# Hyena filters and delta gates: products over 16, 33 and 64 rows made over 128 rows, two passes over the gates' rows made one

## The chip, the cores and the metric

The kernel runs on one core of a Trainium2 chip. The metric is the device time of one execution in microseconds (us); three runs give a median and a spread. PE is TensorE, DVE VectorE, ACT ScalarE, POOL GpSimd, SP the engine whose queue carries the weights' transfers.

## What is computed

Two model blocks follow each other on 256 tokens of 1024 features. The first has two layers, each a gated feed-forward half step, a mixer and a second feed-forward half step. The second has an even mixer with an MLP and an odd mixer with an MLP, and takes a context stream of 256 tokens beside the latent one. The change touches the odd mixer alone. Its two halves are a long convolution whose filters come out of a small network of sines, and a gated delta rule:

```python
def hyena_filters(length, w1, b1, freq1, w2, b2, freq2, w3):
    ...                                           # z: [length, 33]
    hid = jnp.sin(freq1 * (z @ w1 + b1))          # 33 -> 64
    hid = jnp.sin(freq2 * (hid @ w2 + b2))        # 64 -> 64
    filt = (hid @ w3).astype(F32).reshape(length, HY_ORDER, 2, HY_CH)
    filt = filt * jnp.exp(-t * deltas)[:, None, None, :]
    return filt / jnp.sum(jnp.abs(filt), axis=(0, 2), keepdims=True)

def gated_delta_chunked(q, k, v, beta, g, state):   # 4 heads, chunks of 64, both directions
    gcum = jnp.cumsum(g, axis=-1)
    decay = jnp.exp(jnp.where(incl, gcum[..., :, None] - gcum[..., None, :], -jnp.inf))
    lower = jnp.where(strict, jnp.einsum('bhncd,bhnsd->bhncs', kb, k) * decay, 0.0)
    tmat = lax.linalg.triangular_solve(eye + lower, ...)
    ...
    attn = jnp.einsum('bhncd,bhnsd->bhncs', q, k) * decay
```

## The kernel before

Activations lie with the features on the partitions and the tokens on the free axis. A float32 product is made of three float32r passes, high part by high part, high by remainder and remainder by high (`mm3`, L634 to L638). The weights stream once in chunks of six 128x128 tiles: SP's queue brings a chunk into one of four `raw` buffers, ACT rounds it to the high part `whi` (L415), DVE subtracts to get the remainder `wlo` (L416). `whi` and `wlo` have four buffers each (NSPLIT), so ACT can write a chunk's high part only when PE has finished with the chunk four places ahead of it. In the odd mixer a chunk is 18 products where it serves the latent stream.

`hyena_filters` is woven into the second feed-forward layer of the first block, by steps. Both layers of sines (L1404) multiply weights `w1` and `w2` on the partitions 0 to 32 and 0 to 63 alone. The last layer's weights `w3` and the hidden values `hs` stand twice, on the lower and on the upper 64 partitions, with high part and remainder so placed that one pass over 128 rows makes two of the three products; a second pass over 64 rows (L1435) adds the third.

In the odd mixer `delta_gates` makes the running sums `gc` of the gates by token for both streams, transposes them for each stream to 16 rows (block, direction, head; L1562) and copies those to `gcT`. `prep` of each stream (L1609 to L1660) spreads them to four heads' columns of their own (`G`), splits these into `Gh` and `Gl`, and yields. Then for each of two blocks and two directions it makes a row of sums stand on all partitions: a pass with `Gh` (L1634), one with `Gl` (L1635), each over 16 rows, and one with an identity that adds the triangle's mask `fb` (L1636). ACT takes exponentials of the result, four 128x128 tiles `A` (and four `w` in the latent stream).

Each stage of the odd mixer is a generator. The recurrence's are chained as main: `prep1`, then `solve1` and `prep0` by turns, then inverses and states by turns, and `output` at last. The features (projections, short convolutions, SiLU, normalisation) and the long convolution are the filler. `fill` (L361) traces after main's i-th step as many filler steps as the i-th digit of `OD_FILL` says, and what is left at the end. A scheduler then sets each engine's order from what is traced. ACT holds one table of functions at a time, so in its row an exponential behind a SiLU has an ACT_TABLE_LOAD ahead of it, and a SiLU behind an exponential another.

Of the kernel before, what the change touches and what calls it, by code (L numbers as in the profile page):

```python
"""Two model blocks on one core.

Activations live transposed: features on partitions, tokens on the free axis, so the output of
one product is the moving operand of the next. A float32 product is carried by three float32r
passes: each operand is split exactly into a high part (rounded to float32r) and the remainder,
and hi*hi + hi*lo + lo*hi are accumulated in PSUM. Weights stream once from DRAM in the order of
their use. The per-token factor of a root-mean-square norm is applied where a product leaves PSUM.
"""
# [9 lines left out]
F32 = mybir.dt.float32  # L18
F32R = mybir.dt.float32r
AF = mybir.ActivationFunctionType  # L20
ALU = mybir.AluOpType
# [8 lines left out]
CH = 6             # weight tiles of 128x128 in one transfer  # L30
CHM = 4            # the same in the first block's mixers
NRAW, NSPLIT = 4, 4   # transfers and split parts under way
# [6 lines left out]
# parts of the hidden width held on chip at a time  # L39
FFN_PARTS = {(1, 0): 1, (2, 0): 1, (1, 1): 1, (2, 1): 1}  # L40
MLP_PARTS = (4, 2)  # by layer
AHEADW = {"od": 0}  # weight transfers split ahead of their use, by phase (2 otherwise)
ADA = (1.2, 0.8, 1.2)   # steps of the modulation after each of a feed-forward layer's, by layer
AT0 = 4             # first block's attention: the step of the first head's scores,
ATV = 2             # and the steps from a head's scores to its values
# taps of the even mixer's convolution by each engine after a stream's share of its own inputs and of the others
TAPS = ((4.0, 4.0), (2.0, 2.0))
BY = (0, 1, 0, -14)   # the engine of each channel tile; negative: shared, so many taps by the first
MW = 1              # steps from the attention's norm to its transposes
# products traced between the steps of a chain that waits for other engines: so many steps ahead of it and after each  # L50
# of its own; in the even mixer queries, convolution and its outputs between the attention's,
EV_FILL = "2114110100002000031200110015312110300002013"
# in the odd mixer features, long convolution and its outputs between the recurrence's
OD_FILL = ("0000010011200001101310001000000001000100000000000100001011000000000010"
           "00000000001000020001000100000000000011000000001002000010001001114")
FEATS = 8           # steps of the features ahead of the recurrence
BR = (3, 2)         # tiles of each gate of the long convolution ahead of the transform
ODH = 4             # output tiles of the odd mixer that are begun with the long convolution's half
EVH = 2             # the same in the even mixer
SINES = 2           # filters: steps a layer of sines takes,  # L60
HW = 1              # steps from the filters to their transforms,
HF = 1.1            # steps per step of the feed-forward layer
OUTM = 3            # output tiles of the first block's mixers that grow with their inputs,
OUTL = 2            # so many tiles behind
LATE = 2            # output tiles that are begun before the last input tile is there
TS = T + 2         # moving columns with the two of the shift


# ---------------------------------------------------------------- host: layout only
class Cols:  # L70
    """Vectors laid out per partition: a vector of n*128 becomes n columns."""
# [21 lines left out]
def _late(w, ms, ks):  # L93
    """As lins takes them: the last of ks follows the others of the first LATE output tiles."""
    ms, ks = list(ms), list(ks)
    return _blocks(w, ms[:LATE], ks[:-1]) + _blocks(w, ms[:LATE], ks[-1:]) + _blocks(w, ms[LATE:], ks)

# [71 lines left out]
def _tap_cols(w):  # L169
    """[taps, channels] -> [128, channel tile * taps]"""  # L170
    return w.T.reshape(-1, P, w.shape[0]).transpose(1, 0, 2).reshape(P, -1)


def _tlay(x):
    """[tokens, features] -> [128, feature tile, token]"""
    return np.ascontiguousarray(x.T.reshape(-1, P, x.shape[0]).transpose(1, 0, 2))
# [42 lines left out]
def _consts_od():  # L219
# [5 lines left out]
    # allowed entries 0, the others large; i on partitions, j on the free axis  # L225
# [6 lines left out]
    # of the rows (block, direction, head): those of a block and direction, those of a head  # L232
    c["of_bd"] = p[:, None] // 4 == np.arange(4)[None, :]
# [5 lines left out]
def _consts_big():  # L239
    """Over i on partitions and j: allowed entries 0, the others large."""  # L240
    p = np.arange(P)
    le = p[:, None] <= p[None, :]
    return {"f": np.where(le.T, 0.0, 2.0 ** 100), "b": np.where(le, 0.0, 2.0 ** 100)}


def _consts_dft():
    """Real transform of length 512 and its inverse as matrices."""
# [6 lines left out]
    fwd_i[:, 0] = alt                       # row 0 of the imaginary part carries the last frequency  # L254
    c = {}
    dft = np.concatenate([cos, fwd_i], 1)   # [t, 512]
# [9 lines left out]
def _consts_hy():  # L266
    """Transforms of the filters, positional features, decays."""
# [32 lines left out]
def _prep(i):  # L300
    """Arrays of the launch: every one a rearrangement of inputs, or a constant of the shapes."""
# [13 lines left out]
    # second block  # L315
# [33 lines left out]
# ---------------------------------------------------------------- device  # L349
def weave(main, filler, ratio):  # L350
    """Trace main's steps with ratio steps of filler after each; filler goes on behind them."""
    due = 0.0
    for _ in main:
        due += ratio
        while due >= 1.0:
            due -= 1.0
            next(filler, None)
        yield


def fill(main, filler, counts):  # L361
    """Trace main's steps with so many of filler's ahead and after each as the digits of counts say, the rest at last."""
# [7 lines left out]
def both(*gens):  # L370
    """Trace the steps of generators by turns."""
# [14 lines left out]
class Weights:  # L386
    """The stream of 128x128 weight tiles in the order of their use, split on chip ahead of it."""
# [9 lines left out]
    def load(s, n):  # L397
        """The transfers of the chunks before the n-th."""
# [7 lines left out]
    def split(s, n):  # L406
        """The parts of the chunks before the n-th."""
# [12 lines left out]
    def start(s, name):  # L420
        """The phase's first tile comes next."""
# [16 lines left out]
class Split:  # L438
    """An activation operand as high and low float32r parts, [128, tiles, tokens]."""
# [4 lines left out]
    def put(s, nc, k, f):  # L444
        """Split the float32 values f into tile k."""
# [4 lines left out]
class Norm:  # L450
    """x*g split for products, and the per-token factor R (one row, on all partitions).

    With a shift the moving operand has two more columns that hold it: a product's column T is then
    the shift's product, to be added after the factor R.
    """
# [35 lines left out]
    def square(s, k):  # L491
        """The sum of the squares, so far."""
# [11 lines left out]
    def R(s):  # L504
        """Made where it is first asked for, behind the products that were traced before."""
# [6 lines left out]
    def normalise(s):  # L512
        """Of a full norm: the split of x * R * g + shift, a tile at a time."""
# [10 lines left out]
    def apply(s):  # L524
        """Of a plain norm: the factor R, two tiles of x at a time."""
# [5 lines left out]
    def split_all(s, w):  # L531
        """Without the sum of the squares, which is made with R; the first weights w by the way."""
# [6 lines left out]
    def finish(s):  # L539
# [5 lines left out]
        for i, z in enumerate(chain):  # L545
            z.done = n.tp.tile([P, T], F32, tag="R", name="R", bufs=4)
            v = ps[:, i * T:(i + 1) * T]
            if i:
                # the mean square of what the first norm makes
# [8 lines left out]
    def by_token(s):  # L558
        """R with tokens on partitions, a column per block."""
# [9 lines left out]
class Net:  # L569
    def __init__(s, tc, nc, a, at, st):  # L570
# [9 lines left out]
        # the activation table is loaded during the first transfers  # L580
# [31 lines left out]
    def rsqrt(s, v, scale, out=None):  # L612
        """1/sqrt(v*scale + eps)."""
# [9 lines left out]
    def rows(s, rt, d=None):  # L623
        """[128 tokens, blocks] -> PSUM [128, 128 * blocks], the same row of tokens on each partition."""
# [15 lines left out]
    def lin(s, w, sp, ks, ps=None, n=T):  # L640
        """One tile of 128 outputs: [128 features, tokens]."""
# [7 lines left out]
    def lins(s, w, sp, nk, n=T, nm=KD):  # L649
        """nm tiles of outputs, one after the other; see _late."""  # L650
# [11 lines left out]
    def linc(s, w, nrs):  # L662
        """One tile of 128 outputs of the streams' norms with shifts, by one pass over the weights."""
# [10 lines left out]
    def scaled(s, out, ps, nr, func=AF.Identity, scale=1.0):  # L674
        """func(scale * (ps*R + shift)); the shift's product is column T of ps."""
# [11 lines left out]
    def lin_tok(s, w, sp):  # L687
        """512 outputs, tokens on partitions: two blocks of [128 tokens, 512]."""
# [8 lines left out]
    # ---- first block  # L697
# [30 lines left out]
    def consts_of(s, pool, part):  # L728
        """A phase's constants: a function from name to columns."""
# [5 lines left out]
    def rope(s, ps, dst, cosR, sinR, perm):  # L735
        """The first half; the second one, behind the next products, is returned."""
# [14 lines left out]
    def mixer(s, l, nr, nxt):  # L751
        nc, tc = s.nc, s.tc
        w = s.w.start(f"mix_{l}")
        with tc.tile_pool(name=f"mix{l}", bufs=1) as pool, tc.tile_pool(name=f"mixt{l}", bufs=3) as tp:
# [4 lines left out]
            # small inputs  # L759
# [9 lines left out]
            # indexer  # L769
# [3 lines left out]
            nc.scalar.copy(raw, ps)     # 64 rows of the key, 8 of the heads' weights  # L773
# [58 lines left out]
            def select():  # L832
                """One round of eight of the highest scores."""
# [5 lines left out]
            # spatial gating's normalised part  # L839
# [6 lines left out]
            # keys and queries, meanwhile the selection  # L846
# [49 lines left out]
            # attention over the selected keys  # L896
# [86 lines left out]
    # ---- second block  # L983
# [1112 lines left out]
```

## Time and profile before

| | us |
|---|---|
| runs | 2264.89, 2265.63, 2267.83 |
| median | 2265.63 |
| span of the profiled execution | 2263.6 |
| PE busy in it | 2221.3 (98%) |
| DVE busy | 1717.0 (76%) |
| ACT busy | 1295.0 (57%) |
| POOL busy | 76.1 (3%) |

The profiled execution took 2263.6 us by its span, 2.0 us under the median of the runs. PE is busy in 98% of the span and carries 91% of the chain that ended last. Where windows of the profile are shown, each line has the window, its length, the busy time of each engine with the number of instructions, the granted clock of TensorE as a share of 2.4 GHz, and the share of the time in which the DMA engines moved data.

### The profile page before, as it was taken

Reading aid. Unit: us, or ns where it says so; the run is one execution under the profiler, and the core shown is the slowest. Engines: PE = TensorE matmul, PEld = TensorE weight load, DVE = VectorE, ACT = ScalarE, POOL = GpSimd, SP = SyncE. Lnnn points to the kernel's source line nnn. Section 1 sums busy time; section 2 is a strip of 40 time slices with the busy share of each in tenths; the row PEclk is TensorE's granted clock in tenths of the full one; section 3 lists DMA queues with packets and bytes.
Section 4 is the critical chain, followed back from the end, with each engine's and each line's share of the span. In section 5 each row is a group of like instructions: output and inputs, shape, how many; then the busy total and the mean of one; then the engine's idle time right before and its main releaser. Section 6 shows DMA issues by size and latency. Waiting matters only on the chain.

```text
span 2263.6 us, 43627 instructions
## 1 busy us (share of the span) xinstructions
PE 2221.3 (98%) x16752; PEld 2094.1 (93%) x16752; DVE 1717.0 (76%) x3316; ACT 1295.0 (57%) x2475; POOL 76.1 (3%) x114
## 2 busy tenths in 40 slices
PE   8999999999999999999999889999999999999998
PEld 8999899999999999999999867989989898999998
DVE  7877877887688878786768987767764779778565
ACT  6545566655555455675655667625435588437674
POOL 0000000000000000000003800000000000000000
PEclk9999999999999999999999999999999999999999
DMA  7776555776677755466662212456753325224664
GB/s 267 241 229 216 150 160 148 238 213 203 208 239 237 229 176 165 139 206 190 183 186 87 78 43 86 140 166 193 229 174 94 91 66 177 66 62 147 184 185 133
DMA packets 155754, 374.83 MB, mean 166 GB/s; under 512 B 24856, under 2 KB 29720, under 8 KB 155160
## 3 DMA queue, kind: packets, MB, share of 16 engines
q1 hardware_dynamic: 155544, 372.03, 53.2%
q8 instruction: 131, 2.15, 0.4%
q14 instruction: 79, 0.65, 0.1%
HBM read 365.94 MB, written 6.03 MB: 164 GB/s over the span
## 4 chain that ended last, share of the span: by engine, by line
PE 91%; DVE 4%; ACT 3%; DMA 2%; issue 1%; SPq 0%; DVEq 0%; ACTq 0%
PE mm L636 27%; PE mm L637 27%; PE mm L638 27%; DVE ms L1091 1%; DVE wlo L416 1%; DMA raw<-w_ffn 1%; PE ms L1907 1%; PE mm L1882 1%; PE ms L901 1%; PE ms L816 1%; PE ms L1609 1%; PE ms L1700 1%; PE ms L1706 0%; PE ms L743 0%; PE mm L1258 0%
## 5 line engine op out<-in xcount | busy, mean ns | idle before, releaser
L415 ACT ACTIVATE whi<-raw 128x768 fp32r<-128x768 f32 (+1 forms) x840 | 659.0, 787 | 688.5 <-PE mm L637 488.2
L636 PE MATMUL mm<-xh,whi 128*128 128x256 f32 (+1 forms) x3328 | 956.9, 288 | 10.3 <-ACT whi L415 9.4
L638 PE MATMUL mm<-xh,wlo 128*128 128x256 f32 (+1 forms) x3328 | 943.7, 284 | 2.0 <-DVE wlo L416 1.9
L637 PE MATMUL mm<-xl,whi 128*128 128x256 f32 (+1 forms) x3328 | 944.4, 284 | 0.0
L416 DVE TENSOR_TENSOR wlo<-raw,whi 128x768 fp32r<-128x768 f32 (+1 forms) x840 | 746.3, 894 | 260.3 <-ACT whi L415 254.3
L636 PEld LDWEIGHTS mm<-xh,whi 128*128 128x128 f32 x3328 | 633.1, 190 | 23.8 <-ACT whi L415 14.8
L638 PEld LDWEIGHTS mm<-xh,wlo 128*128 128x128 f32 x3328 | 633.3, 191 | 4.2 <-DVE wlo L416 3.7
L637 PEld LDWEIGHTS mm<-xl,whi 128*128 128x128 f32 x3328 | 633.1, 190 | 3.2 <-issue 1.7
L636 PE MATMUL mm<-hh,whi 128*128 128x256 f32 x704 | 197.9, 281 | 0.0
L637 PE MATMUL mm<-hl,whi 128*128 128x256 f32 x704 | 197.6, 281 | 0.0
L638 PE MATMUL mm<-hh,wlo 128*128 128x256 f32 x704 | 197.6, 281 | 0.0
L1001 DVE SCALAR_TENSOR_TENSOR junk<-adaw,cond 128x1024 bf16<-128x1024 f32 x160 | 194.6, 1216 | 1.5 <-DMA adaw<-adaT 1.2
L636 PE MATMUL mm<-mh,whi 128*128 128x512 f32 (+1 forms) x512 | 173.1, 338 | 0.0
L637 PE MATMUL mm<-ml,whi 128*128 128x512 f32 (+1 forms) x512 | 173.1, 338 | 0.0
L638 PE MATMUL mm<-mh,wlo 128*128 128x512 f32 (+1 forms) x512 | 173.1, 338 | 0.0
L636 PEld LDWEIGHTS mm<-hh,whi 128*128 128x128 f32 x704 | 132.7, 188 | 0.6 <-issue 0.5
L637 PEld LDWEIGHTS mm<-hl,whi 128*128 128x128 f32 x704 | 132.7, 188 | 0.1
L638 PEld LDWEIGHTS mm<-hh,wlo 128*128 128x128 f32 x704 | 132.7, 188 | 0.0
L638 PEld LDWEIGHTS mm<-mh,wlo 128*128 128x128 f32 x512 | 96.3, 188 | 11.7
L636 PEld LDWEIGHTS mm<-mh,whi 128*128 128x128 f32 x512 | 96.4, 188 | 11.5
L637 PEld LDWEIGHTS mm<-ml,whi 128*128 128x128 f32 x512 | 96.3, 188 | 11.5
L682 DVE TENSOR_TENSOR t<-mm,R 128x256 f32<-128x256 f32 x154 | 63.7, 417 | 28.7 <-PE mm L638 28.3
(500 smaller groups left out, 2937.7 us busy)
## 6 DMA issues: line engine op xcount, KB each, us to landing
raw<-w_ffn SPq DMA_DIRECT2D x352, 384.0 KB, 3.7
raw<-w_mlp SPq DMA_DIRECT2D x172, 384.0 KB, 3.2
raw<-w_mix SPq DMA_DIRECT2D x228, 256.0 KB, 2.8
adaw<-adaT SPq DMA_DIRECT2D x96, 512.0 KB, 4.2
raw<-w_od SPq DMA_DIRECT2D x50, 384.0 KB, 3.2
raw<-w_ev SPq DMA_DIRECT2D x38, 384.0 KB, 3.1
hyspec<-spec SPq DMA_DIRECT2D x10, 256.0 KB, 2.8
cond<-c SPq DMA_DIRECT2D x4, 512.0 KB, 5.6
```

What stands on the lines that cost most here:

```text
L415: nc.scalar.activation(hi[:, :w], raw, AF.Copy)
L416: nc.vector.tensor_sub(lo[:, :w], raw, hi[:, :w].bitcast(F32))
L636: mm(ps, whi, xhi, start=start, stop=False)
L637: mm(ps, whi, xlo, start=False, stop=False)
L638: mm(ps, wlo, xhi, start=False, stop=stop)
L682: nc.vector.tensor_mul(t, ps[:, :T], R)
L816: nc.tensor.matmul(ps[:, off[b]:off[b] + P * (b + 1)], qi[r0:r0 + 64, h // 2, b * P:(b + 1) * P], ki[r0:r0 + 64, :P * (b + 1)], start=True ...
L901: nc.tensor.matmul(ps[:, b * P:b * P + P * (b + 1)], q_[r0:r0 + 64, h // 2, b * P:(b + 1) * P], k_[r0:r0 + 64, h // 2, :P * (b + 1)], star ...
L1001: nc.vector.scalar_tensor_tensor(junk, w, 1.0, cb[st], op0=ALU.mult, op1=ALU.mult, accum_out=s.mods[st, l][:, m:m + 1])
L1091: nc.vector.scalar_tensor_tensor(acc, v, k, acc, op0=ALU.mult, op1=ALU.add)
L1609: nc.tensor.transpose(v4(pt)[:, h], src[:, h], s.c("ident"))
L1700: mm(half(pz)[:, h], AT[:, h], first(X[:, h]), start=True, stop=True)
```

## The change

The weights of the sines are set to zero first, and their products run over all 128 rows. The filters' second pass runs over 128 rows too: the upper half of `hs` is the remainder and that of `w3l` the weights' remainder, so the fourth, smallest product comes in with it. For the gates one operand holds both streams and both parts: `gx` is zeroed by POOL, gets `gc` of both streams in columns 0 to 31 and again in 64 to 95, and one transpose puts both on partitions; `G2` is the spread of that, with the rounded part on the lower 64 rows and the remainder on the upper ones. It is made once for both streams in `delta_gates`, and `prep` makes one pass over 128 rows where it made two over 16. The `yield` that stood behind the split in `prep` goes, so main has two steps less, while `OD_FILL` is as it was.

```diff
-    c["of_bd"] = p[:, None] // 4 == np.arange(4)[None, :]
+    c["of_bd"] = (p[:, None] % 64) // 4 == np.arange(8)[None, :]
 ... hyena_filters
         w1, w2 = tile([P], "w1"), tile([P], "w2")
+        for t in (w1, w2):
+            nc.gpsimd.memset(t, 0.0)
 ...
-        x, kx = c("zT"), 33
+        x = c("zT")
-            nc.tensor.matmul(ps[:, :T], w[:kx], x[:kx], start=True, stop=True)
+            nc.tensor.matmul(ps[:, :T], w, x, start=True, stop=True)
 ...
                     nc.tensor.matmul(ps, hs[:, t], w3h, start=True, stop=False)
-                    nc.tensor.matmul(ps, hs[:64, t], w3l[:64], start=False, stop=True)
+                    nc.tensor.matmul(ps, hs[:, t], w3l, start=False, stop=True)
 ... delta_gates
-        for st in pss:
-            pg = s.ms()
-            nc.tensor.transpose(pg[:16, :P], gc[:, of[st]].rearrange("p b c -> p (b c)"), s.c("ident"))
-            gcT = pools[st].tile([16, P], F32, name="gcT")
-            nc.scalar.copy(gcT, pg[:16, :P])
+        gx = s.tmp("t2")[:, :P]
+        nc.gpsimd.memset(gx, 0.0)
+        for o in (0, 64):
+            nc.vector.tensor_copy(gx[:, o:o + 8 * n], gc.rearrange("p b c -> p (b c)"))
+        pg = s.ms()
+        nc.tensor.transpose(pg[:, :P], gx, s.c("ident"))
+        gT = s.tmp("t3")[:, :P]
+        nc.scalar.copy(gT, pg[:, :P])
+        G = s.gp.tile([P, 4, P], F32, tag="A", name="G", bufs=2)
+        G2 = s.gp.tile([P, 4, P], F32R, tag="XT", name="G2", bufs=4)
+        nc.vector.tensor_tensor(G, gT[:, None, :].to_broadcast([P, 4, P]), s.od("of_h")[:, :, None].to_broadcast([P, 4, P]),
+                                op=ALU.mult)
+        nc.scalar.copy(G2, G)
+        nc.vector.tensor_sub(G2[64:], G[64:], G2[64:].bitcast(F32))
 ... prep
-            G = gp.tile([16, H, P], F32, tag="A", name="G", bufs=2)
-            nc.vector.tensor_tensor(G, g["gcT"][:, None, :].to_broadcast([16, H, P]),
-                                    s.od("of_h")[:16, :, None].to_broadcast([16, H, P]), op=ALU.mult)
-            Gh, Gl = (gp.tile([16, H, P], F32R, tag="vn", name="G" + n, bufs=2) for n in "hl")
-            nc.scalar.copy(Gh, G)
-            nc.vector.tensor_sub(Gl, G, Gh.bitcast(F32))
-            yield
 ...
-                    one = s.odr["of_bd"][:16, 2 * b + d, None].to_broadcast([16, P])
-                    mm(ps, one, Gh.rearrange("r h t -> r (h t)"), start=True, stop=False)
-                    mm(ps, one, Gl.rearrange("r h t -> r (h t)"), start=False, stop=False)
+                    one = s.odr["of_bd"][:, g["at"] + 2 * b + d, None].to_broadcast([P, P])
+                    mm(ps, one, g["G"].rearrange("r h t -> r (h t)"), start=True, stop=False)
                     mm(v4(ps), s.odr["ident"], s.odr["fb"[d]][:, None, :].to_broadcast([P, H, P]), start=False, stop=True)
```

The order of the whole odd mixer follows from the two steps that main loses. Two places of it are shown. The first is ACT's row where the queries' projection runs on PE (`raw` is a SiLU of a projected tile, `pad` the input of a short convolution, `A` and `w` the exponentials, `qn` the queries' squares, `r` their root, and the transposed `AT` belongs to the context's recurrence). Before:

```order
L415 ACTIVATE whi<-raw 128x768
L1811 ACTIVATE raw<-raw 128x256
L415 ACTIVATE whi<-raw 128x768
...
L685 ACTIVATE pad<-t,sh 128x256
L415 ACTIVATE whi<-raw 128x768 x2
L1811 ACTIVATE raw<-raw 128x256
...
L1575 ACTIVATE qn,ss<-ms 128x128 x8
...
L415 ACTIVATE whi<-raw 128x768
L619 ACT_TABLE_LOAD
L619 ACTIVATE r<-ss,consts 128x8
...
L415 ACTIVATE whi<-raw 128x768
```

After, the latent stream's first exponentials stand in that place:

```order
L415 ACTIVATE whi<-raw 128x768
L1622 COPY AT<-ms 128x512 x2
...
L1644 ACT_TABLE_LOAD
L1644 ACTIVATE A<-ms,gb 128x128
L1814 ACT_TABLE_LOAD
L1814 ACTIVATE raw<-raw 128x256
...
L1644 ACT_TABLE_LOAD
L1644 ACTIVATE A<-ms,gb 128x128 x2
L1644 ACTIVATE w<-ms,gc 128x128 x4
L1587 ACTIVATE qn,ss<-ms 128x128 x8
...
L619 ACTIVATE r<-ss,consts 128x8
...
L415 ACTIVATE whi<-raw 128x768 x3
```

A group's four exponentials `A`, which stood together behind these SiLUs before, now stand one, one and two between them, each piece with a table load ahead of it and another behind, and no `whi` stands between the first row and the last; the rows left out are two more such loads with an exponential and a SiLU, two `pad`, four `sh` and a SiLU.

The second place is PE's row at the recurrence's end (`vn`, `attT` are its last products, `spec` and `hyi` the long convolution's transform back, `cath` the output projection's first half, `on` the normalised output that is transposed). Before:

```order
L1759 MATMUL mm<-vn,attT 128x128 x4
L1907 MATMUL ms<-c_dft,spec 128x256 x2
L1907 MATMUL ms<-c_dft,hyi 128x256 x2
L1759 MATMUL mm<-vn,attT 128x128 x4
L1907 MATMUL ms<-c_dft,spec 128x256 x2
L1907 MATMUL ms<-c_dft,hyi 128x256 x2
L1907 MATMUL ms<-c_dft,spec 128x256 x2
L1907 MATMUL ms<-c_dft,hyi 128x256 x2
L636 MATMUL mm<-cath,whi 128x256
...
L1986 MATMUL ms<-consts,on 128x128 x4
...
L1986 MATMUL ms<-consts,on 128x128 x4
```

After:

```order
L1910 MATMUL ms<-c_dft,spec 128x256 x2
L1910 MATMUL ms<-c_dft,hyi 128x256 x2
L1762 MATMUL mm<-vn,attT 128x128 x8
L1910 MATMUL ms<-c_dft,spec 128x256 x2
L1910 MATMUL ms<-c_dft,hyi 128x256 x2
L636 MATMUL mm<-cath,whi 128x256
...
L636 MATMUL mm<-cath,whi 128x256 x4
L1990 MATMUL ms<-consts,on 128x128 x8
L1910 MATMUL ms<-c_dft,spec 128x256 x2
L1910 MATMUL ms<-c_dft,hyi 128x256 x2
```

Two of the transform's groups that stood ahead of the transposes of `on` now stand behind them.

## Rows read from the trace of the kernel before

**Rows 1.** Windows: busy us of PE, PEld, DVE, ACT, POOL; granted clock; DMA share.
```profile
400.00:580.00 180.00, 178.44 (x1413) 171.41 (x1412) 149.61 (x255) 100.55 (x163) 0.00 (x0) 1.00 0.69 216
1860.00:1900.00 40.00, 37.18 (x271) 33.98 (x271) 33.63 (x78) 34.66 (x83) 0.78 (x12) 0.96 0.51 149
1940.00:2040.00 100.00, 100.00 (x847) 93.62 (x847) 73.03 (x149) 39.43 (x81) 0.33 (x4) 1.00 0.20 55
```

**Rows 2.** PE timeline: start, duration, engine, line, tiles, shape, count [idle before]; filter pair.
```profile
438.75 0.39 PE L1434 MATMUL mm<-w,hids 128*128 128x512 f32 x1
439.07 0.50 PE L1435 MATMUL mm<-w,hids 64*128 64x512 f32 x1
439.50 0.39 PE L636 MATMUL mm<-xh,whi 128*128 128x256 f32 x1
439.72 0.28 PE L637 MATMUL mm<-xl,whi 128*128 128x256 f32 x1
```

**Rows 3.** PE timeline: 128-row products, 512 columns, of the even mixer's feed-forward.
```profile
1472.74 0.40 PE L636 MATMUL mm<-mh,whi 128*128 128x512 f32 x1
1472.98 0.40 PE L637 MATMUL mm<-ml,whi 128*128 128x512 f32 x1
```

**Rows 4.** Line L1435 over the whole span: durations min/median/max, first and last start.
```profile
L1435 PE MATMUL mm<-w,hids x8: 492/493/498, 439.1 to 552.1; 64*128 64x512 f32 x8
```

**Rows 5.** PE timeline: first layer of sines (33 rows) and the next weight product.
```profile
408.47 0.67 PE L1404 MATMUL ms<-c_hy,w 33*128 33x256 f32 x2 [0.35 <-PE mm L638]
409.07 0.39 PE L636 MATMUL mm<-xh,whi 128*128 128x256 f32 x1
```

**Rows 6.** PE timeline: one gate group and the first product of the next.
```profile
1848.80 0.49 PE L1634 MATMUL ms<-Gh,r_of_bd 16*128 16x512 f32 x1
1849.14 0.38 PE L1635 MATMUL ms<-Gl,r_of_bd 16*128 16x512 f32 x1
1849.45 0.50 PE L1636 MATMUL ms<-r_f,r_ident 128*128 128x512 f32 x1
1849.88 0.49 PE L1634 MATMUL ms<-Gh,r_of_bd 16*128 16x512 f32 x1
```

**Rows 7.** Line L1635 over the whole span, as in rows 4.
```profile
L1635 PE MATMUL ms<-Gl,r_of_bd x8: 382/383/393, 1849.1 to 1915.9; 16*128 16x512 f32 x8
```

**Rows 8.** ACT timeline, 1883 to 1906 us.
```profile
1883.98 0.83 ACT L415 ACTIVATE whi<-raw 128x768 fp32r<-128x768 f32 x1
...
1890.39 0.51 ACT L685 ACTIVATE pad<-t,sh 128x256 f32<-128x256 f32 x1
1890.80 0.26 ACT L1575 ACTIVATE qn<-ms 128x128 f32<-128x128 f32 x1
...
1900.95 1.28 ACT L1641 ACT_TABLE_LOAD   x1
1902.25 1.14 ACT L1641 ACTIVATE A<-ms,gb 128x128 f32<-128x128 f32 x4
```

**Rows 9.** DVE timeline: the normalised queries.
```profile
1897.00 1.28 DVE L1580 TENSOR_TENSOR qn<-ms,rt 128x512 f32<-128x512 f32 x2
```

**Rows 10.** A window of 4 us, columns as rows 1: behind PE's idle time.
```profile
1868.00:1872.00 4.00, 4.00 (x20) 3.73 (x19) 3.12 (x6) 3.16 (x7) 0.13 (x2) 0.58 0.58 167
```

**Rows 11.** Timeline of all engines: from the recurrence's last addition to its transposes.
```profile
2041.24 1.03 PE L1907 MATMUL ms<-c_dft,spec 128*128 128x256 f32 x4
2041.44 0.69 DVE L1760 TENSOR_TENSOR o<-o,mm 128x512 f32<-128x512 f32 x1
...
2042.11 1.03 PE L1907 MATMUL ms<-c_dft,hyi 128*128 128x256 f32 x4
...
2043.45 1.28 ACT L619 ACT_TABLE_LOAD   x1
...
2045.72 1.29 DVE L1979 TENSOR_TENSOR on<-o,rt 128x512 f32<-128x512 f32 x2
...
2046.57 0.28 PE L1986 MATMUL ms<-consts,on 128*128 128x128 f32 x1
```

More of the change, by code (lines that the diff above doesn't have):

```diff
@@ L1414, in hyena_filters @@
             nc.scalar.activation(h, a, AF.Sin)
-            x, kx = h, 64
+            x = h
             for _ in range(SINES):
@@ L1558, in delta_gates @@
         nc.vector.scalar_tensor_tensor(bk, beta, -1.0, egc, op0=ALU.mult, op1=ALU.mult)
-        g = {}
-        for st in pss:
-            pg = s.ms()
-            nc.tensor.transpose(pg[:16, :P], gc[:, of[st]].rearrange("p b c -> p (b c)"), s.c("ident"))
-            gcT = pools[st].tile([16, P], F32, name="gcT")
-            nc.scalar.copy(gcT, pg[:16, :P])
-            g[st] = dict(gcT=gcT, **{k: v[:, of[st]] for k, v in dict(beta=beta, gc=gc, gb=gb, egc=egc, bk=bk, kd=kd, egl=egl).items()})
-        yield g
+        gx = s.tmp("t2")[:, :P]
[12 more added lines that the diff above has]
+        nc.vector.tensor_sub(G2[64:], G[64:], G2[64:].bitcast(F32))
+        yield {st: dict(G=G2, at=2 * of[st].start, **{k: v[:, of[st]] for k, v in
+                                                      dict(beta=beta, gc=gc, gb=gb, egc=egc, bk=bk, kd=kd, egl=egl).items()})
+               for st in pss}
     def l2tok(s, src, toks, feat, scale=1.0):
@@ L1949, in odd @@
         od, gp, pool, pc, rp = right.values()
+        s.gp = gp
         s.odd_shared(od)
```

## Prediction

> **What bounds the kernel now.** I read the shares of busy time first (PE 98%), then windows, then the timelines of the two places that the change touches. In the windows [rows 1] the reader sees where the filters are made, at 400 to 580 us: PE is busy for 178.44 of 180 us, with the other engines and the transfers below it. PE time saved there is saved in the end. From 1940 to 2040 us PE is busy without a gap. In between, from 1860 to 1900 us, PE idles for 2.8 of 40 us, while ACT is busy for 34.66: there ACT hands out the parts of the weights in the row in which it stands, and that row decides. So the filters are a question of PE's steps, and the odd mixer one of PE's steps and of the order.
>
> The sum is made against the profiled execution, whose span of 2263.6 us is 2.0 under the median of 2265.6; I take differences and add them to the median. About 0.2%, that is 4.5 us, is what a measurement of this kernel can tell from no change.
>
> **Filters, second pass.** A 128-row product and the 64-row one behind it take 0.32 and 0.43 us from start to start, 0.75 together, and the 256-column product behind them another 0.22 [rows 2]. Two full products of 512 columns follow each other after 0.24 us [rows 3], so a pair would take 0.48, and 0.75 - 0.48 = 0.27 us is saved. At half the columns the product behind should take 0.12 (0.24 / 2) where it takes 0.22, which would make it 0.37. There are eight pairs [rows 4]: 2.2 to 3.0 us, and I take 3.0, as the slow step stands at every change between narrow and full.
>
> **Filters, sines.** The 33-row layer takes 0.60 us to the next product [rows 5]. Full float32 products of 256 columns are recorded as pairs too: four records take 0.87 us [rows 11], two 0.43. That saves 0.17 us a layer, with 0.10 for the product behind 0.27; two layers make 0.3 to 0.5. I take 0.5. The two fills of zeros are on POOL, which is idle here [rows 1], ahead of the weights' transfers, whose wait is before the first layer; should it show, it is some tenths once. Filters together: -2.5 to -3.5, and I take **-3.5**, all on PE's path.
>
> The Trainium skill, "TensorEngine Tiling (Array Packing)", section Performance Considerations, says to tile the rows where the contraction is 64 or less, which speaks against filling them up. It lets narrow products run beside each other; here each narrow one has a full one ahead and behind. By that rule padding would bring nothing, as in rival 4; [rows 2] against [rows 3] say otherwise. The same page, section Key Properties, says that a change of tiling mode drains the engine, which agrees with the slow steps there [rows 2].
>
> **Gates, PE.** A group of three passes takes 1.08 us to the next [rows 6]; two full ones would take 0.48 [rows 3]. That is 0.60 for each of eight groups [rows 7], 4.8 us of PE time. How much of it counts depends on the place. The first four groups stand where PE waits for ACT soon after, at 1860 us [rows 1], so PE would only wait longer: I count -0.2, with the single transpose in place of two. Two are in the stretch told next (-1.2 there). Two come in the last stretch, where PE is all but full: **-1.2**. The work that replaces the small operands, a POOL fill, two copies, one spread and one split for both streams instead of two, is less than what goes, and lies ahead of the exponentials on the way to them: 0 to +0.3, in the -0.2.
>
> **Order, queries' stretch.** PE can go four chunks past the point at which ACT writes a `whi`: 4 x 18 products, 0.12 us each, 8.6 us, and what stands between them. In the order after, that is eight transposes of `A`, four products for `kT`, two gate groups, eight and four transposes, which I put at 4.5 us: 13.1 us of PE work. On ACT there stand between this `whi` and the next, by the order: six table loads at 1.30 from start to start, eight exponentials at 1.14 / 4, eight squares at 0.26, three SiLUs and three `pad` at about 0.4, two copies of 512 columns that I put at 0.55 (by the 768 of `whi` in 0.83) and some small ones [rows 8]. In us: 7.8 + 2.3 + 2.1 + 2.4 + 1.1 + 0.4 = 16.1, with two `whi` at the ends 17.6. Some overlap of neighbours brings it to about 17.2. PE then waits for **4 us or more**. DVE has its own row behind `r`: normalised queries, 1.28 [rows 9], and short convolutions of about 0.4 each, then `wlo`. That makes the wait up to 6.5. Before, PE idled for 2.8 us in all of 1860 to 1900 [rows 1], some 1.9 of it behind the first gates. After an idle stretch the granted clock went to 0.58 for 4 us [rows 10], a loss of 1.7; it may or may not come here. So: +4 to +6.5, -1.9, -1.2 for two groups, 0 to +1.7, **+0.9 to +5.1**, and I take +3.2.
>
> The Trainium skill, "ScalarE: Activation LUTs", section What ACT_TABLE_LOAD costs, gives 2.66 us for each change of table, with a drain behind the load. In [rows 8] the first exponential starts 1.30 us after its load. By the page the six loads would take 8.2 us more, and the time would be 2274; the rows leave that no chance of its own.
>
> **Order, the recurrence's end.** Here the chain from the recurrence's last addition (2041.44) runs over squares, a table load and a scaling to the transposes of `on` (2046.57), 5.1 us [rows 11]. Behind the last `attT` two groups of the transform back (0.87 for `spec`, as much for `hyi`, 1.74 a group [rows 11]) and fifteen products of `cath` (0.12 each) covered it: 5.3 us. By the order after, one group and sixteen products stand there, 1.74 + 1.9 = 3.6 us, and two groups go behind the transposes. The wait is 5.1 - 3.6 = **1.5 us**, 0 to 2.5. In between the latent state and inverse steps stand closer in PE's row, so that an addition (0.69 [rows 11]) or two of those lies bare; there was no idle time before from 1940 us on [rows 1]. I put that at 0 to +2, and take +1.
>
> **The sum:** -3.5 -0.2 -1.2 +3.2 +1.5 +1.0 = +0.8, that is 2266.4, and I say **2266**. The ends: -4.9 +0.9 +0 +0 = -4.0, 2261.6, and -3.9 +5.1 +2.5 +2 = +5.7, 2271.3.
>
> **Rivals.**
> 1. The waits don't come: ACT's row is shorter than I sum up, or PE's work between covers it. Then the filters' 3.5 and the gates' 4.8 both count: -8.3, 2257. For it: PE is busy in 98% of the span. Against: ACT was the later engine in that place before [rows 1]. Half of it, with a wait of 2 to 3 us left, gives 2260 to 2261.
> 2. Slower: ACT's row with six table loads starves PE of `whi` and `wlo` in the queries' stretch with its full price, 6.5 + 1.7 - 3.1 = 5.1, and the end's chain lies bare too (2.5 + 2). -4.9 + 5.1 + 2.5 + 2 = +4.7, 2270.3, and up to 2271.3 with the filters at their low end. With the end's terms in full it decides from a net price of the queries' stretch of about 4.9 on, that is a way of 20 us or more over ACT and DVE from one chunk to the next against PE's 13, and the slower clock behind it.
> 3. The filters alone count, and order and gates in the odd mixer balance: -3.5, 2262.
> 4. The change doesn't do what it says: the slow steps [rows 2, 6] come from new operands, not from the narrow rows, and stay. Then the filters' and gates' terms are gone (3.5 + 0.2 + 1.2 + 1.2): 0.8 + 6.1 = +6.9, 2272.5. Against it: a full product behind a full one makes 0.24 [rows 3], a narrow one never.
>
> **How the numbers follow.** My forecast, with stalls about as summed (2262 to 2270): 0.50. Rival 1: 0.18 (0.10 for its whole, 0.08 for half). Rival 2: 0.15. Rival 3: 0.13. Rival 4: 0.04. Faster than 2261.1 are all of rival 1 and a share of rival 3 and of the forecast's low edge, 0.18 + 0.04 + 0.04 = 0.26. Slower than 2270.1 are rivals 2 and 4 and the forecast's high edge, less a quarter of rival 2 that ends below: 0.11 + 0.04 + 0.05 = 0.20. Same is 0.54. The range goes from 2259 to 2271.5: whole rival 1 is left out below (0.10) and the worst of rival 2 and 4 above (0.10).
>
> **What would show it.** After, eight pairs at L1435 with steps of about 0.24 and 400 to 580 us shorter by 3 to 4: the filters are right. Two gate passes 0.48 us a group. In the queries' stretch a row of `PE mm <- ACT whi` or `DVE wlo` of 4 to 6.5 us, with the clock below 1 behind it or not: the order is right; none there means rival 1. An idle time of 1 to 2 us ahead of the transposes of `on`. The forecast is wrong if the odd mixer becomes shorter, or if a wait of over 2 us shows at another place.

## The result: 0.7% slower, and where the time went

The changed kernel takes 2280.59 us (median of 4 runs, 2274.81 to 2284.57), the kernel before 2265.26 beside it: a ratio of 1.0071, with an interval of 1.0059 to 1.0083, so 16 us slower. The profiled execution has a span of 2279.9 us against 2263.6.

The products did what they should. The filters' stretch on PE, start, duration, line, shape:

```profile
438.58 0.39 PE L1436 MATMUL mm<-w,hids 128*128 128x512 f32 x1
438.81 0.39 PE L1437 MATMUL mm<-w,hids 128*128 128x512 f32 x1
439.04 0.28 PE L636 MATMUL mm<-xh,whi 128*128 128x256 f32 x1
439.16 0.28 PE L637 MATMUL mm<-xl,whi 128*128 128x256 f32 x1
```

The pair takes 0.23 + 0.23 = 0.46 us where it took 0.75, and the product behind it 0.12 where it took 0.22 [rows 2]. That is 0.39 us for each of eight pairs, 3.1 us. When I follow the weight products one by one through both traces, those behind the filters come 3.16 us earlier than before. The sines have no part in it: the weight products are 0.19 us early ahead of their two layers (406 us) and 0.17 behind them (438 us); the first layer's shorter step is met by a longer wait ahead of it (0.54 us against 0.35). A gate group has two passes now:

```profile
1847.78 0.48 PE L1638 MATMUL ms<-G,r_of_bd 128*128 128x512 f32 x1
1848.09 0.40 PE L1639 MATMUL ms<-r_f,r_ident 128*128 128x512 f32 x1
1848.33 0.40 PE L1638 MATMUL ms<-G,r_of_bd 128*128 128x512 f32 x1
1848.56 0.39 PE L1639 MATMUL ms<-r_b,r_ident 128*128 128x512 f32 x1
```

The first group takes 0.55 us, the second is as short as the filters' pair, where one took 1.08 [rows 6]. All the loss lies between 1820 and 2064 us, in the odd mixer: a weight product at 1800 us comes 0.83 us earlier than before (an attention stretch ahead has given part of the filters' gain back in this one execution), and at 2080 us 16.25 us later. The windows of the changed kernel, columns as in [rows 1]:

```profile
1860.00:1900.00 40.00, 29.17 (x197) 26.39 (x196) 34.10 (x82) 37.77 (x89) 0.65 (x10) 0.85 0.40 106
1940.00:2040.00 100.00, 95.24 (x766) 88.16 (x765) 68.79 (x147) 36.75 (x75) 0.39 (x6) 0.97 0.17 48
```

From 1860 to 1900 us PE idles for 10.8 of 40 us (2.8 before), and the stretch from 1940 to 2040 us, full before, has 4.8 us of idle time. The view of waits names them. PE's waits of the changed kernel from 1800 to 2064 us: line, what it waits for, us in total, times, the longest:

```profile
PE ms L1638 <- DVE qn L1592: 5.7, 1, 5.7
PE ms L1621 <- DVE w L1656: 2.7, 1, 2.7
PE ms L1725 <- DVE Z L1721: 2.1, 1, 2.1
PE ms L1506 <- ACT raw L1814: 1.9, 1, 1.9
PE ms L1597 <- ACT A L1644: 1.5, 1, 1.5
PE ms L1506 <- ACT w L1644: 1.4, 1, 1.4
PE ms L1621 <- DVE w L1692: 1.4, 1, 1.4
PE ms L1506 <- ACT A L1644: 1.2, 2, 0.7
PE mm L1755 <- DVE A L1742: 1.2, 1, 1.2
PE mm L636 <- ACT cath L446: 0.9, 1, 0.9
```

With two small ones that are not shown these come to 20.5 us; the same view of the kernel before has 3.7. That is 16.8 us more. Behind some of the longer waits the granted clock falls: in 1880 to 1900 us it is 0.78, in 2000 to 2020 us 0.83, where both windows had 1.00 before; 0.22 x 20 + 0.17 x 20 makes at most 7.8 us more, and without the time in which PE idles anyway some 6 (an estimate from the windows of 4 us shown at the end). The shorter passes take 4 to 5 us off. The three together give about 18 us, where the odd mixer lost 17.1 (0.83 + 16.25).

The largest wait. PE's row in the queries' stretch:

```profile
1889.28 0.66 PE L1506 MATMUL ms<-consts,raw 128*128 128x128 f32 x4 [1.44 <-ACT w L1644]
1895.60 0.77 PE L1638 MATMUL ms<-G,r_of_bd 128*128 128x512 f32 x1 [5.66 <-DVE qn L1592]
...
1896.58 1.06 PE L1597 MATMUL ms<-consts,qn 128*128 128x128 f32 x4
```

ACT's row at the same time:

```profile
1879.45 1.28 ACT L1644 ACT_TABLE_LOAD   x1
1880.75 0.37 ACT L1644 ACTIVATE A<-ms,gb 128x128 f32<-128x128 f32 x1
1881.14 1.28 ACT L1814 ACT_TABLE_LOAD   x1
1882.43 0.42 ACT L1814 ACTIVATE raw<-raw 128x256 f32<-128x256 f32 x1
...
1891.43 1.28 ACT L619 ACT_TABLE_LOAD   x1
1892.73 0.30 ACT L619 ACTIVATE r<-ss,consts 128x8 f32<-128x8 f32 x1
...
1893.73 2.29 ACT L415 ACTIVATE whi<-raw 128x768 fp32r<-128x768 f32 x3
```

And DVE's, where the root `r` goes on:

```profile
1894.02 0.39 DVE L1676 TENSOR_REDUCE t<-t 128x15 f32<-128x225 f32 x1
1894.33 0.19 DVE L620 RECIPROCAL rt<-r 128x8 f32<-128x8 f32 x1
1894.55 0.17 DVE L1590 TENSOR_SCALAR rt<-rt 128x8 f32<-128x8 f32 x1
1894.76 1.29 DVE L1592 TENSOR_TENSOR qn<-ms,rt 128x512 f32<-128x512 f32 x2
```

ACT is busy without a gap; six table loads stand between 1879.45 and the root at 1892.73, each 1.30 us from its start to the next instruction. DVE takes `r` up 1.3 us after its end, right behind the last step of the context's solve (L1676). A gate group that wants the PSUM bank which the queries' transposes hold, and the transposes of `qn` behind it, stand in PE's row ahead of the next weight products, so it is the normalised queries, not `whi`, that end the wait. The difference is small: the first of ACT's three `whi` is there at about 1894.5 us (1893.73 + 2.29 / 3, an estimate), some 1.1 us before PE goes on.

### The profile page after: what moved, and what is told of

It is laid out like the page before. It is cut to its first block, busy times and chain, and to the rows that moved or that the text cites. A ratio compares the mean times of both kernels' runs of the same rounds, so it can differ in the third digit from the quotient of the medians.

```text
span 2279.9 us, 43624 instructions
## 1 busy us (share of the span) xinstructions
PE 2221.6 (97%) x16743; PEld 2100.7 (92%) x16743; DVE 1719.5 (75%) x3316; ACT 1299.4 (57%) x2476; POOL 76.6 (3%) x117
## 4 chain that ended last, share of the span: by engine, by line
PE 88%; DVE 6%; ACT 3%; DMA 2%; issue 1%; SPq 0%; DVEq 0%; ACTq 0%; POOLq 0%
PE mm L636 26%; PE mm L637 26%; PE mm L638 26%; DVE ms L1091 2%; DVE wlo L416 1%; PE ms L1703 1%; PE ms L1709 1%; PE mm L1885 1%; PE ms L816 1%; PE ms L901 1%; PE ms L1621 1%; PE ms L1910 1%; PE mm L1258 1%; PE ms L743 0%; ACT L619 0%
## 5 line engine op out<-in xcount | busy, mean ns | idle before, releaser
L636 PEld LDWEIGHTS mm<-xh,whi 128*128 128x128 f32 x3328 | 633.8, 190 | 20.5 <-ACT whi L415 13.3
```

The source lines that it names most:

```text
L636: mm(ps, whi, xhi, start=start, stop=False)
```

## The experiments

All times are compared with the kernel before on the same chip; us in the text are the ratio's difference from 1, times 2265. Beside the runs the kernel before took 2263.3 to 2264.5 us, while the expectations start from 2265.3, so it is 2265.3 and this difference that are held against them. The intervals reach 2 to 4 us to either side, so a difference between two of the changed kernels is known to about 4 us.

| run | what it has | ratio (interval) | us from before |
|---|---|---|---|
| changed kernel | all | 1.0071 (1.0059 to 1.0083) | +16.1 |
| e1 | filters alone | 0.9989 (0.9979 to 0.9999) | -2.5 |
| e7 | gates alone, steps as before | 0.9989 (0.9980 to 0.9998) | -2.5 |
| e2, e8 | filters and gates, steps as before | 0.9992 (0.9979 to 1.0004), 0.9975 (0.9966 to 0.9984) | -1.8, -5.7 |
| e3 | before, steps taken out | 1.0092 (1.0077 to 1.0108) | +20.8 |
| e4 | changed, latent's step back | 1.0018 (1.0008 to 1.0028) | +4.1 |
| e9 | changed, context's step back | 1.0029 (1.0018 to 1.0040) | +6.6 |
| e5 | changed, step behind latent's prep | 1.0045 (1.0029 to 1.0060) | +10.2 |
| e6 | changed, step ahead, one less behind | 1.0041 (1.0027 to 1.0054) | +9.3 |
| e10 | changed, no SiLU of the queries | 1.0032 (1.0020 to 1.0043) | +7.2 |

The first theory was that the lost steps did it: `prep` yields once less for each stream, `OD_FILL` still counts the old steps, so everything behind stands otherwise against the filler. The rival was that the wide operands did it: `G2` in the ring of the XT buffers, and one chain for both streams ahead of the first exponentials.

**e1, the filters alone.** The kernel before with

```diff
+        for t in (w1, w2):
+            nc.gpsimd.memset(t, 0.0)
 ...
-            nc.tensor.matmul(ps[:, :T], w[:kx], x[:kx], start=True, stop=True)
+            nc.tensor.matmul(ps[:, :T], w, x, start=True, stop=True)
 ...
-                    nc.tensor.matmul(ps, hs[:64, t], w3l[:64], start=False, stop=True)
+                    nc.tensor.matmul(ps, hs[:, t], w3l, start=False, stop=True)
```

> The kernel before with the filters' edit alone: zeroed w1 and w2, sines and second pass over 128 rows. Nothing of the odd mixer changes. In the changed kernel the weight products behind the filters came 3.16 us earlier than before, at 600 us of the span. Both theories (the loss is the odd mixer's order; the loss is the odd mixer's wide operands) expect 2265.3 - 3.2 = 2262.1, or up to 1 or 2 us later where a later stretch that waits for something else gives a part back.

Measured: 2263.38 us, ratio 0.9989, 2.5 us less (0.2 to 4.8). The weight products behind the filters come 2.85 us earlier, and 3.3 at 1800 us. From 1840 us on it is 4.85, for the granted clock did not fall at 1824 us in this execution, as it did in the profiled one of the kernel before; so the part beyond 3.3 can't be put down to the edit. The gain is real and near the 3.2 expected.

**e2, the changed kernel with both steps back.**

```diff
             g = f["g"]
+            yield
             for b in range(2):
```

> The changed kernel with an empty step put back at the start of prep, so that main has as many steps as before and each digit of OD_FILL falls on the same stage. All products and operands stay as in the changed kernel. Theory order: the loss of 15 us came from the steps; the time falls to 2265.3 - 3.2 (filters) - 1 to 4.8 (gates) = 2257 to 2261. Theory operands (the wide G2 takes one of the four XT buffers until the last gate group, one chain for both streams): it stays at 2275 or above.

Measured: 2262.03 us, ratio 0.9992, that is 2263.5 against the expected 2257 to 2261; above the range, and not told from no change, but 18 us below the changed kernel. All wide products and operands are in it. The rival falls: the operands don't cost the time.

**e3, the steps out of the kernel before.**

```diff
             nc.vector.tensor_sub(Gl, G, Gh.bitcast(F32))
-            yield
```

> The kernel before, with the one yield in prep deleted and nothing else: narrow products, two passes, operands of 16 rows. Theory order: the odd mixer loses what it lost in the changed kernel, 17 us, and with the narrow gates perhaps 1 to 4 more: 2278 to 2287. Theory operands: 2263 to 2268.

Measured: 2284.06 us, ratio 1.0092, 20.8 us slower (17.4 to 24.5). One deleted line with a `yield`, a step less in each stream's prep, and no other edit, makes the whole loss and more. Its waits are of the same kind, the largest 5.3 us at the gate group in the queries' stretch. The changed kernel is 4.7 us better than this one, by its shorter products.

**e4, the latent stream's step back alone.**

```diff
             g = f["g"]
+            if st == 0:
+                yield
```

> The changed kernel with the empty step put back for the latent stream's prep alone; main has one step less than before. Theory order with the queries' stretch as its main price (exponentials between the SiLUs, six table loads): ACT's row has 55 table loads in place of 60 and the stretch loses its 7 us of waits and its slower clock, about 2268 to 2271. Theory order with the price spread over inverses and states: 2274 to 2280. Theory operands: 2275 or above.

Measured: 2266.85 us, ratio 1.0018: 12 us below the changed kernel, and by the ratio 2269.4, within what was expected of the queries' stretch alone. The time can't tell more; its waits of PE can. The one for `Z` is 0.3 us, those for `A` and `cath` are gone, so this step holds more than that stretch.

**e5, the step behind the latent stream's prep** instead of ahead of it, so that the queries' stretch stays as it is and the stages behind stand as with e4.

```diff
                         atts[i, d] = transpose_to(f["ap"].tile(...), decs[d])
                     yield
+            if st == 0:
+                yield
```

> The changed kernel with one empty step put behind the end of the latent stream's prep. ACT's and PE's rows up to there stay as in the changed kernel, exponentials among the SiLUs included; the inverses and states that follow come one step later against the filler. Theory two places (of the 15 us that the latent step is worth, the queries' stretch costs about 10 and the inverses and states about 6): 2280.6 - 6 = 2275, and the waits of PE for DVE's Z, w and A behind 1940 us go while the 5.7 us for the normalised queries stays. Theory one place (all of it follows from the queries' stretch): 2279 to 2281.

Measured: 2273.21 us, ratio 1.0045, 5.9 us below the changed kernel. Its waits of PE, from 1800 to 2064 us:

```profile
PE ms L1638 <- ACT whi L415: 5.5, 1, 5.5
...
PE ms L1621 <- DVE w L1656: 1.3, 1, 1.3
...
PE ms L1727 <- DVE Z L1723: 0.3, 1, 0.3
```

The long wait in the queries' stretch is still there (the profile puts the same gate group's wait down to ACT's `whi`, which runs at the same time as `qn`; the group does not read it); the waits for `Z` and `A` behind 1940 us and the one for `cath` are gone or small. The wait for `w` in the latent stream's prep, 2.7 us in the changed kernel, is 1.3 as well, so the 5.9 us are not of the inverses and states alone.

**e6, the mirror image.**

```diff
             g = f["g"]
+            if st == 0:
+                yield
 ...
-                    yield
+                    if st or b == 0 or d == 0:
+                        yield
```

> The mirror image: the empty step at the start of the latent stream's prep, and the last yield of that prep taken away, so that the stages behind it stand against the filler as in the changed kernel. ACT has 55 table loads. Theory two places: the queries' stretch loses its price of about 10, the waits behind 1940 us stay: 2280.6 - 9 = 2271 to 2273. Theory one place: as with the step alone, 2267.

Measured: 2273.49 us, ratio 1.0041, 6.8 us below the changed kernel and by the ratio 2274.6, a little above the range for two places. Its waits of PE, same stretch:

```profile
PE ms L1728 <- DVE Z L1724: 2.1, 1, 2.1
...
PE ms L1621 <- DVE w L1695: 1.4, 1, 1.4
PE ms L1640 <- ACT pad L685: 1.2, 1, 1.2
PE mm L1758 <- DVE A L1745: 1.2, 1, 1.2
PE mm L636 <- ACT cath L446: 0.9, 1, 0.9
```

Here the queries' wait is 1.2 us, and 2.1, 1.4, 1.2 and 0.9 behind 1935 us are as in the changed kernel. The two parts make 5.9 + 6.8 = 12.7 us, the whole step 12.0 (e4). Within the 4 us to which such differences are known, the loss of the latent step sits in two places; which is the larger is not shown.

**e9, the context's step back alone** (the diff of e4 with `st == 1`).

> The changed kernel with the empty step put back for the context's prep alone. With both steps the time is 2258 to 2262, with the latent one alone 2267. If the two steps' prices add, the context's step is worth 5 to 9 of the changed kernel's 2280.6: 2272 to 2276. Its order has 59 table loads, one less than the changed kernel. If the first step moves everything behind it to another alignment that is as bad, 2278 or above.

Measured: 2270.43 us, ratio 1.0029, 9.5 us below the changed kernel, by the ratio 2271.9, at the low end of what was expected. With the latent's 12.0 that makes 21.5, and with both back 17.9 (e2) to 21.8 (e8) were gained. So the prices add within what the runs scatter, but not because the steps have places of their own. In e9's waits the 5.7 us for the normalised queries is gone, `Z` is 0.3, and `A` and `cath` are gone, the same as in e4. In all traces the wait at the queries is 5.3 to 5.7 us where both steps are missing ahead of it (changed kernel, e3, e5), and none to 1.2 where one is there (e4, e6, e9); that for `Z` is 2.0 to 2.1 us where both are missing (changed kernel, e3, e6, e10), and 0.3 where one is (e4, e5, e9). (e10, where both are missing too but the loads are gone, has 1.2 us at the queries.) In these runs both large places show only where both steps are missing. What one lost step alone leaves is elsewhere, the largest a wait of 3.5 (e4) and 3.2 us (e9) for `w` in the latent stream's prep, 0.5 and 0.6 with both steps back.

**e10, the table loads.** The changed kernel, with a copy in place of SiLU for the latent queries, so that ACT changes no table between the exponentials:

```diff
-                nc.scalar.activation(y, y, AF.Silu)
+                nc.scalar.activation(y, y, AF.Silu if len(nrs) > 1 else AF.Copy)
```

> The changed kernel with a plain copy in place of SiLU for the latent stream's queries, so the output is not the reference's; steps and digits stay as in the changed kernel. ACT then needs no change of table between the exponentials: 56 loads in place of 60, 4 x 1.30 = 5.2 us less in the queries' stretch, and the scheduler puts a whi between again and the normalised queries' transposes later. Theory loads (the price of about 10 there comes from the exponentials and SiLUs changing tables): the 5.7 us wait for the normalised queries is under 1 us, and the time is 2270 to 2274, with the waits behind 1940 us still there. Theory solve (DVE's row of the context's solve holds the queries' root, whatever ACT does): the wait stays at 4 us or more, 2277 to 2281.

Measured: 2270.54 us, ratio 1.0032, 8.9 us below the changed kernel. In its view of PE's waits:

```profile
PE ms L1725 <- DVE Z L1721: 2.0, 1, 2.0
...
PE ms L1638 <- DVE qn L1592: 1.2, 1, 1.2
```

The wait for the queries falls from 5.7 to 1.2 us, where under 1 was expected, and the later ones stay. So in the queries' stretch the exponentials and SiLUs that stand in turns on ACT's row make most of the price, not the context's solve on DVE. With fewer loads the scheduler also puts a `whi` between and PE's transposes of the queries later; the loads' own 5.2 us and that shift were not separated.

**e7 and e8, the edits' own worth.** e7 is e2 without the filters' lines, e8 is e2 measured again.

> The gates' edit without the filters' and with the empty step in both streams' prep, so that main's steps count as before. By the prediction's steps, 0.60 us for each of eight groups of which four lie where PE waits for ACT: 1.4 to 2.6 us less than before, 2262 to 2264. If all eight counted: 2260.5. If the single chain for both streams delays the first exponentials by more than the passes save: 2265 or above.

> The kernel with both edits and the empty steps put back, a second time and in more rounds, beside the gates' edit alone on the same chip. The filters' edit should stand between the two with its 3.2 us: 2259 to 2261, and 4 to 6 us below the kernel before.

Measured: e7 2260.96 us, 0.9989, 2.5 us less (0.5 to 4.5); e8 2257.98 us, 0.9975, 5.7 us less (3.6 to 7.7). The gates' edit is worth about 2.5 us, the filters' as much, and together 1.8 (e2, not told from none) to 5.7 us below the kernel before. The windows of e8:

```profile
1860.00:1900.00 40.00, 37.70 (x293) 36.56 (x294) 35.29 (x87) 35.86 (x92) 0.90 (x12) 0.96 0.66 206
1940.00:2040.00 100.00, 100.00 (x835) 93.57 (x834) 72.07 (x150) 41.17 (x89) 0.26 (x4) 1.00 0.18 54
```

They are those of the kernel before [rows 1] again, with 37.7 us of PE work in 1860 to 1900 and no idle time from 1940 to 2040.

## Why the prediction was wrong

It said 2266 us, 2259 to 2271.5; it was 2280.6, outside the range and on the side that had 0.20. The time of the changed kernel lies beyond its worst rival, 2272.5. Its own sign of being wrong came true too: waits of over 2 us stand at other places, 2.7 us for `w` in the latent stream's prep and 2.1 us for `Z`.

**Filters, -3.5: right.** 0.39 us for each pair against 0.37 forecast, 3.16 us in the trace, 2.5 by e1. The 0.5 us for the sines in it did not come; the pairs' 3.0 did (from 0.17 us early at 438 us to 3.16 at 600). The Trainium skill's page "TensorEngine Tiling (Array Packing)", section Performance Considerations, would tile such rows; the trace decides for full rows here, 0.46 against 0.75 us for the pair. Its drain at a change of mode, section Key Properties, agrees with the slow step of the full product behind a narrow one (0.22 against 0.12 us).

**Gates, -2.6 where they count: right.** About 0.58 us a group against 0.60, and 2.5 us by e7. As forecast, the first groups' gain went into PE's wait for ACT: before the context's key transposes it is 1.5 us, with the steps back (e2, e8) too, and 0.4 before.

**Order, queries' stretch, +3.2 (0.9 to 5.1): right in mechanism, too small.** The loads were priced rightly (1.30 us each in the trace), and ACT's way from one `whi`'s start to the next's nearly so: 17.6 us (1876.12 to 1893.73) against 16.9 by the sum. e6 makes the place 6.8 us, e10 8.9 with the loads gone. Three parts of the working failed. I credited 1.9 us of idle time of before against it, but that idle stood behind the first gates and did not go: in that place the waits grew, to 4.9 us. I let the wait end with `whi` and `wlo`, 4 to 6.5 us; it ended with the normalised queries, behind ACT's root and DVE's solve, 1.44 + 5.66 = 7.1 us. And for the clock I had 1.7 us at most, from one stretch of 4 us, where the granted clock was at 0.50 for the eight us from 1892 on; from 1896 to 1904 that is 2.6 us (4 x 0.50 + 4 x 0.16). By the Trainium skill, "ScalarE: Activation LUTs", section What ACT_TABLE_LOAD costs, a change of table takes 2.66 us; the trace of this kernel has 1.30 from load to next instruction, as [rows 8] had, and does not agree.

**Order, inverses and states, +1 (0 to 2): this step failed.** In the changed kernel's trace these stages hold waits of 2.06, 1.40 and 1.20 us, 4.7 together, and 3.0 us of slower clock behind the last two. e5, which undoes them, takes 5.9 us off, with the 0.9 of the recurrence's end and a part of the wait for `w` among it. I had no row of idle time there and took one or two additions as the price. What hid the chains before was filler that stood between their steps. Before, PE's row has, in the context's first inverse:

```profile
1936.99 0.97 PE L1716 MATMUL ms<-w,AT 128*64 128x64 f32 x16
1937.89 1.13 PE L1907 MATMUL ms<-c_dft,spec 128*128 128x256 f32 x4
1938.86 1.03 PE L1907 MATMUL ms<-c_dft,hyi 128*128 128x256 f32 x4
1939.82 0.96 PE L1722 MATMUL ms<-XT,Z 64*64 64x64 f32 x16
```

and the changed kernel has the same two steps with nothing between:

```profile
1943.55 0.97 PE L1719 MATMUL ms<-w,AT 128*64 128x64 f32 x16
1946.58 1.34 PE L1725 MATMUL ms<-XT,Z 64*64 64x64 f32 x16 [2.06 <-DVE Z L1721]
```

One pair of the long convolution's transform, 1.9 us, covered the copy of `Z`; in the new order it stands behind. DVE's row has changed with it: its first copy of `Z` starts 0.1 us after the products of L1716 end in the kernel before, and 1.5 us after those of L1719 in the changed one, behind other work of DVE. How much of the 2.06 us is due to either was not separated. Every such place of the new order had to be looked up, not one end of it.

**The recurrence's end, +1.5: half right.** 0.9 us, and not ahead of the transposes of `on` but one instruction earlier, where the remaining products wait for `cath`. In ACT's row the last `cath` stands behind the squares, the table load and the root of that chain (2057.04 to 2058.54 us). It goes in e5 with the rest of that step.

**What was not priced: the context's step.** The prediction treated the two lost steps by what the latent stream's exponentials do, and gave the first groups -0.2. Putting it back alone takes 9.5 us off (e9), for in these runs the two large places show only where both steps are missing. Of the rivals, number 2 had the right mechanism at the queries and at the end alone; the range was built on one large wait, and there were several. e3 says what the order alone costs: 20.8 us, where the terms of the order made 5.7, or 6.9 without the 1.2 us of the gates that stand in the first.

## What to carry to other kernels

A list of counts that says what is traced behind which step belongs to the steps: an edit that drops a yield shifts every digit behind it, and here that cost four times what the edit saved. Keep an empty step in its place (e2 and e8), or move the digits with it (not run here), and compare the engines' rows before anything is timed. When an order changes as a whole, price each pair of dependent instructions that now stand next to each other on the busiest engine; a stretch without any idle time before says only that something covered them.

## What the runs showed of the hardware

A wait can cost more than its length. After the two waits of 1.44 and 5.66 us the granted clock went to 0.50, and stayed there beyond the wait; after those of 1.40 and 1.20 us, too. Windows of 4 us of the changed kernel, columns as in [rows 1]:

```profile
1892.00:1896.00 4.00, 0.41 (x1) 0.44 (x2) 3.76 (x11) 3.99 (x7) 0.00 (x0) 0.50 0.15 49
1896.00:1900.00 4.00, 3.73 (x15) 3.14 (x15) 4.00 (x9) 3.95 (x11) 0.26 (x4) 0.50 0.33 33
1900.00:1904.00 4.00, 4.00 (x30) 4.00 (x30) 2.77 (x6) 2.48 (x5) 0.00 (x0) 0.84 0.80 223
...
1912.00:1916.00 4.00, 1.72 (x16) 1.48 (x14) 2.29 (x5) 2.25 (x5) 0.13 (x2) 1.00 0.40 155
...
1944.00:1948.00 4.00, 1.91 (x29) 1.60 (x27) 3.91 (x13) 0.45 (x1) 0.13 (x2) 1.00 0.37 102
...
2008.00:2012.00 4.00, 4.00 (x20) 4.00 (x21) 1.61 (x4) 0.59 (x1) 0.00 (x0) 0.50 0.00 0
2012.00:2016.00 4.00, 4.00 (x28) 4.00 (x28) 2.48 (x4) 1.51 (x3) 0.00 (x0) 0.76 0.02 6
2016.00:2020.00 4.00, 4.00 (x37) 4.00 (x36) 3.16 (x7) 2.18 (x4) 0.00 (x0) 1.00 0.51 131
```

From 2008 to 2012 us PE is busy all the time at 0.50, which is 1.2 GHz, and gets 20 instructions done where the window from 2016 to 2020 us has 37. From 2008 to 2016 the clock takes 4 x 0.50 + 4 x 0.24 = 3.0 us, more than the two waits of 2.6 us together. But the length of a wait does not settle it. The single waits of 2.75 us, at 1914, and of 2.06 us, at 1945, left the clock at 1.00 in this trace, while in e3 the same 2.06 us for `Z` stands in a stretch of 0.91 (1940 to 1960 us), and in e2 one wait of 2.2 us in one of 0.91 (1880 to 1900 us). In the kernel before, waits of under 0.7 us at a time from 1880 on left the clock at 1.00.
